# Running sums of squares by adding transfers instead of GpSimd additions

## The chip, the cores and the metric

The kernel runs on one core of a Trainium2 chip. A core has five engines with instruction queues of their own: TensorE (PE in the profile; its weight loads are listed as PEld), VectorE (DVE), ScalarE (ACT), GpSimd (POOL) and SyncE (SP, which here only issues transfers). The metric is the device time of one execution in microseconds; the kernel before takes 1895.79 us.

## The reference

A decoder trunk of two layers over 512 tokens of width 1024. Each layer has a channel mixer, a token mixer and a second channel mixer, each behind a norm of its own:

```python
def rmsnorm(x, g):
    x32 = x.astype(jnp.float32)
    y = x32 * lax.rsqrt(jnp.mean(x32 * x32, axis=-1, keepdims=True) + RMS_EPS)
    return y.astype(x.dtype) * g

def swiglu(x, w_gate, w_up, w_down):
    return (jax.nn.silu(x @ w_gate) * (x @ w_up)) @ w_down

for i in range(DEPTH):                     # DEPTH = 2
    h = h + 0.5 * swiglu(rmsnorm(h, ffn_norm_a[i]), ...)
    m = rmsnorm(h, mix_norm[i])
    h = h + mixer_i(m)                     # 0: latent attention (MLA), 1: sparse attention (NSA)
    h = h + 0.5 * swiglu(rmsnorm(h, ffn_norm_b[i]), ...)
return rmsnorm(h, final_norm)
```

The hidden width of a channel mixer is 2816. Everything is float32.

## The kernel before

**Layout.** The residual stream stays in SBUF as eight chunks `h[0]` to `h[7]`, each 128 features (partitions) by 512 tokens. Products run on TensorE in three passes: each operand is split into a high part, written by ACT, and a low part, the rest, written by DVE (`split`, L173 and L174 with a gain; `wslab`, L143 and L145 for weights).

**The norm.** A norm has two halves. The gain is multiplied into the split of each chunk as soon as the chunk is done (`norm_split`). The root of the mean square comes later, as a factor on the outputs of the products, since it is one number per token. For it the squares of the eight chunks have to be added: `sumsq` squares a chunk on ACT (L250) and adds it to the running sum `s2` on POOL (L254). Then `norm_col` adds over the partitions with small matmuls into `pc` (L276), DVE takes the inverse root by Newton steps on 128x4 numbers (`newton`, L264 to L269), and `norm_bcast` spreads it over the partitions into `pb` (L288), which ACT copies to `row`.

**The order.** The chunks come out one by one at the end of the previous mixer, in `w_o1` for a token mixer (`h` by L629) and at the end of `ffn` for a channel mixer (`h` by L399). `norm_chunk` is called for each. For a norm ahead of a channel mixer (gains b0, a1, b1; `to_ffn`) the last two chunks of the order are put into `late`: their squares are taken inside the next `ffn`.

**The channel mixer.** `ffn(idx, ...)` goes over 22 blocks of 128 hidden features. The first three (`PLAIN`) are computed directly: block `f` has a gate projection `pg` and an up projection `pu`, both by `plain` (L362 to L364), 48 matmuls each. From the fourth block on seven products stand in place of eight; `wsums` loads its weights (`rg` by L315, `ru` by L317) and `combine` builds the sums of activations for them, with ACT copies `y` (L232) and DVE differences `u` (L236 to L238). The root is needed after the two projections of the second block, where `row` enters the gates. The call `late()` in `ffn` adds the last two squares and calls `norm_col`: for `idx` 1 behind the up projection of the first block, for `idx` 2 and 3 between its two projections. `idx` 0 takes its root in another way.

**Memory and queues.** Squares are written to a scratch tile `sq`. In the token mixers it shares six buffers with the attention's `p` tiles; in `ffn` it has one buffer. Each mixer has memory pools of its own, which are opened when it begins and given back when it ends, so the first tiles of a mixer lie where the previous mixer's tiles were. Each engine takes its instructions in one fixed order. That order is not the order of the text: the build draws it from the dependences and its own estimates of durations, and breaks ties by the order of the text.

Transfers are issued by SP (weights) and ACT (constants, output); POOL issues none. In this kernel POOL adds squares, makes some low parts during the attention and scales probabilities.

Of the kernel before, what the change touches and what calls it, by code (L numbers as in the profile page):

```python
# [11 lines left out]
F32 = mybir.dt.float32  # L12
F32R = mybir.dt.float32r
I32 = mybir.dt.int32
AF = mybir.ActivationFunctionType
ALU = mybir.AluOpType
AX = mybir.AxisListType

P = 128
S = 512  # L20
D = 1024
# [40 lines left out]
class Kern:  # L62
# [112 lines left out]

    def norm_begin(self, gain):
        self.ng = GAINS[gain] if gain else None
        self.xh, self.xl, self.s2, self.late = [], [], None, []
        self.to_ffn = gain in FGAINS
        self.nng = 8 * FGAINS.index(gain) if self.to_ffn else None  # L180
        self.xc = {}

        self.order = [c + KP * e for c in range(KP) for e in range(2)] if self.to_ffn and gain != "a0" else list(range(KC))

    def norm_chunk(self, c):

        self.norm_split(c)
        if self.to_ffn and c in self.order[-2:]:

            self.late.append(c)  # L190
        else:
            self.sumsq(self.h[c], self.s2 is None)

    def norm_split(self, c):
        t = self.xp.tile([P, 2 * S], F32R, tag="x", bufs=KC, name="x")
        if self.to_ffn:

            g = self.ngains[:, self.nng + c : self.nng + c + 1]
            v = t.rearrange("p (e z n) -> p e z n", e=2, z=2)
            hi, lo, src = v[:, :, 0, :], v[:, :, 1, :], self.h[c].rearrange("p (e n) -> p e n", e=2)  # L200
            self.split(src, hi, lo, gain=g)
            for e in range(2):
                self.xc["LR"[e], c] = v[:, e, 0, :], v[:, e, 1, :]
        else:
            self.split(self.h[c], t[:, :S], t[:, S:], gain=self.gains[:, self.ng + c : self.ng + c + 1])
            self.xh.append(t[:, :S])
            self.xl.append(t[:, S:])
# [157 lines left out]

    def ffn(self, idx, gain_next, ap, tp):
        nc, a = self.nc, self.a
        self.scr, self.fp = (tp, "sq", 1), tp
        ah, al, ht, row = {}, {}, [], None
        tg, tu, units = {}, {}, []  # L370

        def gate(f, g):

            t = tg[f] = tp.tile([P, S], F32, tag="tg", bufs=2, name="tg")
            nc.vector.tensor_tensor(t, g, row, op=ALU.mult)
            nc.scalar.activation(t, t, AF.Silu, scale=-1.0)
            nc.vector.tensor_tensor(t, t, row, op=ALU.mult)
# [4 lines left out]
        def act(f):  # L382
            t = tu[f]
            if f < PLAIN:
                t = tu_tile()
                nc.vector.scalar_tensor_tensor(t, tu[f], -1.0, tg[f], op0=ALU.mult, op1=ALU.mult)
            else:
                nc.vector.tensor_tensor(t, t, tg[f], op=ALU.mult)
            ah[f] = ap.tile([P, S], F32R, tag="act", bufs=4 * NG, name="ah")
            al[f] = ap.tile([P, S], F32R, tag="act", bufs=4 * NG, name="al")  # L390
            self.split(t, ah[f], al[f])
# [21 lines left out]
        def tokens(t):  # L413

            xts.append(tp.tile([P, D], F32, tag="fr", bufs=3, name="xt"))
            with self.tc.issue_after(self.high.ins):
                nc.scalar.dma_start(xts[t], a["x_tok"][t * P : (t + 1) * P, :])

        def squares(t):
            nc.scalar.activation(xts[t], xts[t], AF.Square, accum_out=sums[:, t : t + 1])  # L420

        def late():
            for c in self.late:
                self.sumsq(self.h[c])
            return self.norm_col(D, self.s2)

        if idx == 0:
            for t in range(3):
                tokens(t)


        gates = [self.bank("T", "pg") for _ in range(PLAIN)]
        for f, g in enumerate(gates):
            u = tu[f] = self.bank(("mm", "S")[f % 2], "pu")
            self.plain(idx, f, 0, g)
            if f == 0 and idx > 1:
                col = late()
            if f == 1 and idx == 0:

                squares(0)  # L440
                tokens(3)
                squares(1)
            self.plain(idx, f, 1, u)
            if f == 0 and idx == 1:

                col = late()
            if f == 1:
                if idx == 0:
                    squares(2)
                    squares(3)  # L450
                    col = self.rsqrt_col(sums, D)
                pb = self.norm_bcast(col)
                row = tp.tile([P, S], F32, tag="row", bufs=1, name="row")
                nc.scalar.activation(row, pb, AF.Copy)
                for e in range(2):
                    gate(e, gates[e])
                    act(e)
            elif f:
                gate(f, g)
                act(f)  # L460
            for p in (((0,), (1,), (2, 3)) if idx else ((0, 1), (2,), (3,)))[f]:
                self.combine(p)
# [875 lines left out]
```

## Time and profile before

| | |
|---|---|
| median of three runs | 1895.79 us |
| fastest run | 1895.11 us |
| span of the profiled execution | 1891.5 us |
| own time of the profiled execution | not listed; median less span is 4.3 us |
| TensorE busy | 1865.3 us, 99% of the span |
| VectorE busy | 1527.3 us, 81% |
| ScalarE busy | 1091.4 us, 58% |
| GpSimd busy | 291.8 us, 15% |
| additions of squares on GpSimd (L254) | 38, mean 1441 ns, 54.8 us |

How to read the rows. In a timeline: start and duration in us, engine, line of the code, operation, output tile `<-` input tiles, shapes, count; in brackets how long the engine stood idle before it and what released it. A row of a group gives the count, the total time, the mean of one in ns, and the idle time before. In a windows table each engine's busy time stands with its number of instructions. `SPq` is SyncE's queue of transfers. Matmuls overlap in TensorE's pipeline, so their durations are longer than the distance of their starts.

### The profile page before, as it was taken

To read this page: it belongs to the slowest core of one execution; us is meant where nothing else is said; L and a number is where in the kernel's file an instruction comes from. 1 tells how busy PE (TensorE), PEld (TensorE's weight loads), DVE (VectorE), ACT (ScalarE), POOL (GpSimd) and SP (SyncE) were. 2 spreads that over 40 slices of the span, in tenths; PEclk is the share of its full clock that TensorE was granted. 3 is DMA by queue.
4 is the path that set the end of the run, shared out by engine and by line. 5 is a ranking of instruction groups with operands and counts; after the bars stand their busy time and mean duration, and the time that the engine had idled before them with its cause. 6 is when DMAs were issued, how large, how long until landed. Compare 5 with 4: busy or idle time off the path is not lost.

```text
span 1891.5 us, 33006 instructions
## 1 busy us (share of the span) xinstructions
PE 1865.3 (99%) x12510; PEld 1696.1 (90%) x12510; DVE 1527.3 (81%) x2884; ACT 1091.4 (58%) x2031; POOL 291.8 (15%) x351
## 2 busy tenths in 40 slices
PE   8999999999999999999999999999999999999998
PEld 8999999878879999998999999988788889999997
DVE  8988886677779888886988888666988989888885
ACT  7555554478756555554655555435887866555553
POOL 0000000257720000001100000032666530000000
PEclk9999999999999999999999999999999999999999
DMA  6433331311133333322433332143122133333321
GB/s 231 138 101 100 103 99 41 112 54 46 59 105 117 113 108 105 101 75 60 162 105 101 108 113 87 43 148 106 57 65 70 34 120 117 110 107 107 102 77 67
DMA packets 75903, 183.26 MB, mean 97 GB/s; under 512 B 9041, under 2 KB 37073, under 8 KB 75745
## 3 DMA queue, kind: packets, MB, share of 16 engines
q1 hardware_dynamic: 72800, 176.39, 29.7%
q10 hardware_dynamic: 2944, 4.77, 0.7%
q8 instruction: 98, 1.61, 0.4%
q14 instruction: 61, 0.49, 0.1%
HBM read 178.96 MB, written 2.16 MB: 96 GB/s over the span
## 4 chain that ended last, share of the span: by engine, by line
PE 85%; DVE 7%; ACT 5%; issue 2%; POOL 1%; DMA 1%; SPq 0%; DVEq 0%; ACTq 0%; POOLq 0%
PE pd L163 8%; PE pd L162 8%; PE pd L164 8%; PE px L350 5%; PE px L351 5%; PE px L352 5%; PE pg L350 4%; PE pg L352 4%; PE pg L351 4%; PE pq L352 4%; PE pq L350 4%; PE pq L351 4%; ACT p L643 1%; PE o L1149 1%; PE po L162 1%
## 5 line engine op out<-in xcount | busy, mean ns | idle before, releaser
L163 PE MATMUL pd<-al,wd 128*128 128x512 f32 x576 | 225.0, 391 | 0.0
L162 PE MATMUL pd<-ah,wd 128*128 128x512 f32 x576 | 224.8, 390 | 0.0
L164 PE MATMUL pd<-ah,wd 128*128 128x512 f32 x576 | 224.6, 390 | 0.0
L254 POOL TENSOR_TENSOR s<-s,sq 128x512 f32<-128x512 f32 x38 | 54.8, 1441 | 1062.6 <-ACT sq L250 1059.5
L171 DVE TENSOR_TENSOR w<-wr,w 128x1024 fp32r<-128x1024 f32 x72 | 88.1, 1224 | 135.5 <-ACT w L170 135.5
L350 PE MATMUL px<-four,wh 128*128 128x256 f32 x608 | 168.6, 277 | 0.1
L352 PE MATMUL pq<-four,wl 128*128 128x256 f32 x608 | 167.9, 276 | 0.3 <-DVE wl L171 0.3
L352 PE MATMUL px<-four,wl 128*128 128x256 f32 x608 | 168.0, 276 | 0.0
L350 PE MATMUL pq<-four,wh 128*128 128x256 f32 x608 | 167.9, 276 | 0.0
L351 PE MATMUL px<-four,wh 128*128 128x256 f32 x608 | 167.9, 276 | 0.0
L351 PE MATMUL pq<-four,wh 128*128 128x256 f32 x608 | 167.8, 276 | 0.0
L399 DVE SCALAR_TENSOR_TENSOR h<-pd,h 128x512 f32<-128x512 f32 x216 | 147.5, 683 | 13.9 <-PE pd L164 13.8
L143 ACT ACTIVATE w<-wr 128x1024 fp32r<-128x1024 f32 (+5 forms) x120 | 100.6, 844 | 97.5 <-issue 19.6
L170 ACT ACTIVATE wd<-wdr 128x384 fp32r<-128x384 f32 x192 | 99.2, 519 | 98.5 <-ACT wd L170 63.0
L164 PEld LDWEIGHTS pd<-ah,wd 128*128 128x128 f32 x576 | 108.2, 188 | 22.9
L162 PEld LDWEIGHTS pd<-ah,wd 128*128 128x128 f32 x576 | 108.1, 188 | 20.3
L163 PEld LDWEIGHTS pd<-al,wd 128*128 128x128 f32 x576 | 108.1, 188 | 19.6
L145 DVE TENSOR_TENSOR w<-wr,w 128x1024 fp32r<-128x1024 f32 (+4 forms) x81 | 84.2, 1041 | 49.2 <-ACT w L143 48.5
L643 ACT ACTIVATE p<-p,small 128x512 f32<-128x512 f32 (+2 forms) x192 | 106.5, 556 | 19.8 <-DVE small L642 16.9
L171 DVE TENSOR_TENSOR wd<-wdr,wd 128x384 fp32r<-128x384 f32 x192 | 105.2, 550 | 14.8 <-ACT wd L170 13.9
L350 PEld LDWEIGHTS px<-four,wh 128*128 128x128 f32 x608 | 114.1, 188 | 1.3 <-ACT pg L481 0.8
L170 ACT ACTIVATE w<-wr 128x1024 fp32r<-128x1024 f32 x72 | 76.5, 1062 | 66.4 <-PE pg L352 62.4
(348 smaller groups left out, 6243.9 us busy)
## 6 DMA issues: line engine op xcount, KB each, us to landing
wr<-in_w_gu SPq DMA_DIRECT2D x96, 512.0 KB, 3.3
ru<-in_w_gu SPq DMA_DIRECT2D x76, 512.0 KB, 4.1
wdr<-in_w_down SPq DMA_DIRECT2D x192, 192.0 KB, 2.4
wr<-in_w_down SPq DMA_DIRECT2D x24, 256.0 KB, 2.6
wr<-in_mla_w_o SPq DMA_DIRECT2D x8, 512.0 KB, 3.3
wr<-in_nsa_w_q SPq DMA_DIRECT2D x8, 512.0 KB, 3.3
th<-btab_d SPq DMA_DIRECT2D x16, 256.0 KB, 3.5
wr<-in_nsa_w_o SPq DMA_DIRECT2D x8, 512.0 KB, 3.5
```

Source lines behind the costliest of these rows:

```text
L143: self.copied = nc.scalar.activation(wh[:, m], raw[:, m], AF.Copy)
L145: nc.vector.tensor_tensor(wl[:, m], raw[:, m], f32v(wh[:, m]), op=ALU.subtract)
L162: mm(out, wh, xh, start=first, stop=False)
L163: mm(out, wh, xl, start=False, stop=False)
L164: return mm(out, wl, xh, start=False, stop=last)
L170: nc.scalar.activation(hi, src, AF.Copy)
L171: (nc.gpsimd if pool else nc.vector).tensor_tensor(lo, src, f32v(hi), op=ALU.subtract)
L350: mm(out, wh[:, p], xh, start=first and p == 0, stop=False, skip_group_check=True)
L351: mm(out, wh[:, p], xl, start=False, stop=False, skip_group_check=True)
L352: mm(out, wl[:, p], xh, start=False, stop=last and p == KP - 1, skip_group_check=True)
L399: nc.vector.scalar_tensor_tensor(self.h[c], p, 0.5, self.h[c], op0=ALU.mult, op1=ALU.add)
L643: nc.scalar.activation(p_sb[:, :n], p_sb[:, :n], AF.Exp, bias=nm, scale=-1.0, accum_out=sm)
```

## The change

The three norms ahead of channel mixers that follow another mixer (b0, a1, b1) no longer use `sumsq`. A new `squares` keeps two running sums, `sums2[0]` and `sums2[1]`. The first square of each is written straight into it by ACT. Each further square goes to a scratch tile, and a transfer issued by POOL, with `accum_op=add`, adds it to one of the two sums in turn. The two late squares are moved to the head of the next `ffn`, ahead of its first weights. `late()` adds the two sums on DVE and calls `norm_col`; for `idx` 2 and 3 the call moves from between the projections of the first block to behind them, where it already stood for `idx` 1. The scratch tile in `ffn` gets three buffers in place of one. The norms ahead of the token mixers, and those inside MLA, keep `sumsq`.

```diff
     def norm_begin(self, gain):
         self.ng = GAINS[gain] if gain else None
-        self.xh, self.xl, self.s2, self.late = [], [], None, []
+        self.xh, self.xl, self.s2, self.late, self.nsq = [], [], None, [], 0
         self.to_ffn = gain in FGAINS
         self.nng = 8 * FGAINS.index(gain) if self.to_ffn else None
-        self.xc = {}
+        self.xc, self.sums2 = {}, []
...
             self.late.append(c)
+        elif self.to_ffn:
+            self.squares(c)
         else:
             self.sumsq(self.h[c], self.s2 is None)
+
+    def squares(self, c):
+
+        nc, z = self.nc, self.nsq % 2
+        self.nsq += 1
+        if len(self.sums2) < 2:
+            self.sums2.append(self.sp.tile([P, S], F32, tag="s2", bufs=2, name="s2"))
+            nc.scalar.activation(self.sums2[z], self.h[c], AF.Square)
+        else:
+            sq = self.scratch("sq")
+            nc.scalar.activation(sq, self.h[c], AF.Square)
+            nc.gpsimd.dma_start(self.sums2[z], sq, accum_op=ALU.add)
...
     def ffn(self, idx, gain_next, ap, tp):
         nc, a = self.nc, self.a
-        self.scr, self.fp = (tp, "sq", 1), tp
+        self.scr, self.fp = (tp, "sq", 3), tp
...
         def late():
-            for c in self.late:
-                self.sumsq(self.h[c])
-            return self.norm_col(D, self.s2)
+            nc.vector.tensor_tensor(self.sums2[0], self.sums2[0], self.sums2[1], op=ALU.add)
+            return self.norm_col(D, self.sums2[0])
...
+        for c in self.late if idx else []:
+            self.squares(c)
         gates = [self.bank("T", "pg") for _ in range(PLAIN)]
         for f, g in enumerate(gates):
             u = tu[f] = self.bank(("mm", "S")[f % 2], "pu")
             self.plain(idx, f, 0, g)
-            if f == 0 and idx > 1:
-                col = late()
...
             self.plain(idx, f, 1, u)
-            if f == 0 and idx == 1:
-
+            if f == 0 and idx:
                 col = late()
```

## The prediction

> **What bounds the kernel now.** I read the head of the page first, then the group of the instructions that the change replaces, then three windows around the three norms that it touches.
>
> ```profile
> span 1891.5 us, 33006 instructions
> ...
> PE 1865.3 (99%) x12510; PEld 1696.1 (90%) x12510; DVE 1527.3 (81%) x2884; ACT 1091.4 (58%) x2031; POOL 291.8 (15%) x351
> ...
> L254 POOL TENSOR_TENSOR s<-s,sq 128x512 f32<-128x512 f32 x38 | 54.8, 1441 | 1062.6 <-ACT sq L250 1059.5
> ```
>
> TensorE is busy for 1865.3 of 1891.5 us. Whatever the change does, it can give back at most the idle 26.2 us, 1.4% of the span, and only the share of it that stands near a norm. The POOL additions cost 54.8 us in all, but POOL is idle for most of the span: their own time is on nobody's path.
>
> ```profile
> core 0: us, PE busy (x) PEld busy (x) DVE busy (x) ACT busy (x) POOL busy (x), PEclk, DMA share, GB/s
> 545.00:592.00 47.00, 44.37 (x309) 40.32 (x307) 42.18 (x63) 31.87 (x45) 10.22 (x7) 1.00 0.44 143
> 882.00:930.00 48.00, 46.98 (x323) 43.05 (x322) 40.02 (x65) 32.38 (x47) 10.55 (x7) 1.00 0.50 163
> 1526.00:1570.00 44.00, 43.96 (x314) 40.72 (x313) 40.33 (x63) 32.49 (x45) 9.98 (x7) 1.00 0.48 163
> ```
>
> These are the norms ahead of the second, third and fourth channel mixer (I call them b0, a1 and b1 after their gains). TensorE is idle for 2.63, 1.02 and 0.04 us there, 3.69 us together. That is the ceiling of the gain. The timeline of TensorE in these windows names each gap in its last column:
>
> ```profile
> 561.55 0.39 PE L364 MATMUL pg<-x,w 128*128 128x256 f32 x1 [0.58 <-DVE w L145]
> 566.74 0.38 PE L362 MATMUL pg<-x,w 128*128 128x256 f32 x1 [0.35 <-ACT x L173]
> 567.78 0.38 PE L363 MATMUL pg<-x,w 128*128 128x256 f32 x1 [0.66 <-DVE x L174]
> 573.94 0.94 PE L276 MATMUL pc<-ones,s 128*128 128x1 f32 x8
> 575.45 0.39 PE L364 MATMUL pg<-x,w 128*128 128x256 f32 x1 [0.22 <-DVE w L145]
> 581.95 0.39 PE L364 MATMUL pu<-x,w 128*128 128x256 f32 x1 [0.77 <-DVE w L145]
> ...
> 903.07 0.39 PE L364 MATMUL pg<-x,w 128*128 128x256 f32 x1 [0.75 <-DVE w L145]
> 908.27 0.39 PE L363 MATMUL pg<-x,w 128*128 128x256 f32 x1 [0.27 <-DVE x L174]
> 908.98 0.95 PE L276 MATMUL pc<-ones,s 128*128 128x1 f32 x8
> 926.24 1.05 PE L288 MATMUL pb<-ident,small 128*128 128x128 f32 x8
> ```
>
> The matmuls that read the sum (pc, L276) and those that spread its root (pb, L288) carry no gap: the norm itself is never late. The gaps are waits for VectorE's splits of weights (L145) and of the activations (L174). Why is VectorE late there? Its own rows, two by line for 530 to 600 us (min/median/max) and four by time:
>
> ```profile
> L174 DVE SCALAR_TENSOR_TENSOR x<-h,ngains,x x8: 737/752/1774, 548.4 to 567.0; 128x512 fp32r<-128x512 f32 x8
> ...
> L145 DVE TENSOR_TENSOR w<-wr,w x9: 1209/1220/1700, 538.0 to 588.6; 128x1024 fp32r<-128x1024 f32 x9
> ...
> 555.32 1.77 DVE L174 SCALAR_TENSOR_TENSOR x<-h,ngains,x 128x512 fp32r<-128x512 f32 x1
> 559.96 1.53 DVE L145 TENSOR_TENSOR w<-wr,w 128x1024 fp32r<-128x1024 f32 x1
> 561.42 1.77 DVE L174 SCALAR_TENSOR_TENSOR x<-h,ngains,x 128x512 fp32r<-128x512 f32 x1
> ...
> 906.44 1.78 DVE L174 SCALAR_TENSOR_TENSOR x<-h,ngains,x 128x512 fp32r<-128x512 f32 x1
> ```
>
> ```profile
> 554.94 1.60 POOL L254 TENSOR_TENSOR s<-s,sq 128x512 f32<-128x512 f32 x1 [0.63 <-ACT sq L250]
> 561.26 1.38 POOL L254 TENSOR_TENSOR s<-s,sq 128x512 f32<-128x512 f32 x1 [0.85 <-ACT sq L250]
> ...
> 898.71 1.34 POOL L254 TENSOR_TENSOR s<-s,sq 128x512 f32<-128x512 f32 x1 [1.37 <-ACT sq L250]
> 903.01 1.82 POOL L254 TENSOR_TENSOR s<-s,sq 128x512 f32<-128x512 f32 x1 [2.97 <-DVE w L145]
> ```
>
> The long L174 instructions (1.77 beside a median of 0.75) lie over POOL additions: 555.32 beside 554.94, 561.42 beside 561.26. The addition at 903.01 was held 2.97 us by VectorE in its turn. So the two engines hold each other up when both read two operands, and in b0 that costs VectorE 1.02 + 0.31 + 1.02 = 2.35 us in the row of instructions that ends in the gaps 0.58, 0.35 and 0.66.
>
> **What the change removes.** Each touched norm loses seven POOL additions (window column POOL: x7), 21 of the 38. In b0 the three gaps sum to 1.59 us; 2.35 us of VectorE delay stand ahead of them, so I count all 1.59 as gone. The two later gaps, 0.22 and 0.77, come from a VectorE that works off its backlog; it is relieved, but gets a new addition (below), so I count half, 0.50. In a1 the 0.27 hangs on the long instruction at 906.44 and goes. In b1 TensorE has no gap to lose.
>
> The squares change no count: eight ACT squares per norm before and after. The buffer of the squares in the mixers grows from one to three. The one wait that this ends is the 0.47 in the second row here, ACT time behind which no TensorE gap stands; I cost it at nothing.
>
> ```profile
> 568.90 0.63 ACT L250 ACTIVATE sq<-h 128x512 f32<-128x512 f32 x1 [0.47 <-POOL s L254]
> ...
> 898.01 0.62 ACT L250 ACTIVATE sq<-h 128x512 f32<-128x512 f32 x1
> 900.08 0.72 ACT L232 ACTIVATE y<-h,gains 128x512 f32<-128x512 f32 x1 [1.45 <-POOL s L254]
> 900.71 1.04 ACT L143 ACTIVATE w<-wr 128x1024 fp32r<-128x1024 f32 x1
> ```
>
> **What it adds.** Six transfers per norm, 18 in all, issued by POOL, each 256 KB from SBUF into SBUF with an addition. The trace has no transfer issued by POOL and none that adds, so I bound the time L from the end of the square to the landing by the nearest transfers (last column: us to landing):
>
> ```profile
> th<-btab_d SPq DMA_DIRECT2D x16, 256.0 KB, 3.5
> ...
> h<-in_x SPq DMA_DIRECT2D x8, 256.0 KB, 5.0
> ...
> out_t<-four SPq DMA_DIRECT2D x4, 256.0 KB, 2.0
> ...
> w<-in_nsa_w SPq DMA_DIRECT2D x2, 0.5 KB, 8.3
> ```
>
> Between 2.0 (256 KB out of SBUF) and 8.3 us (the slowest kind in the program) I take 3.5, the row of the same size in the middle of the kernel. The Trainium skill, page "DMA: Bandwidth & Descriptors", section on the anatomy of one DMA on the gpsimd path, gives such a transfer about 2.0 us plus its bytes at 436 GB/s; for 256 KB that is an estimate of 2.6 us by the page. No run here shows it yet; by it the release worked out next would come 1.2 us later than now, not 2.1.
>
> First new wait: the old scratch memory. In a1 the copy y (L232), the first write into the new mixer's memory, waits until 900.05 for the POOL addition of the sixth square (898.71 + 1.34); so does the load rg. In b0 rg follows the addition that ends at 562.64.
>
> ```profile
> 562.66 0.33 SPq L315 DMA_DIRECT2D rg<-in_w_gu  x1
> ...
> 900.07 0.33 SPq L315 DMA_DIRECT2D rg<-in_w_gu  x1
> ```
>
> After the change both wait for a landing: in a1 898.63 + 3.5 = 902.1, that is 2.1 us later. Queued behind y on ACT is the weight copy of 900.71, on which the gap of 0.75 hangs; behind rg on SP are ru and the next weight loads. If the build keeps that order, a1 loses 2.1 us. But y stands far behind the weight copy in the program's text and was drawn ahead when the build took it for ready early; with a later release I expect the weight copy ahead. Then the 0.75 shrinks, but the first late square, which the new code puts ahead of this copy, may take its place on ACT (0.62 us, on the row of 898.01). I count 0.23 of the 0.75, with the 0.27 a gain of 0.50 in a1. In b0 rg moves to 561.26 + 3.5 = 564.8, with ru behind it; VectorE's first sum that uses ru is this:
>
> ```profile
> 571.24 0.68 DVE L336 TENSOR_TENSOR s<-ru 128x512 f32<-128x512 f32 x1
> ...
> 910.69 0.14 DVE L259 TENSOR_SCALAR small<-pc 128x4 f32<-128x4 f32 x1
> ...
> 919.71 0.15 DVE L269 SCALAR_TENSOR_TENSOR small<-small 128x4 f32<-128x4 f32 x1
> ```
>
> 564.8 plus 5.0 for a load in traffic is 569.8, ahead of 571.24: hidden.
>
> Second: one VectorE addition per norm, 0.68 us by L336, three of them. It is hidden by VectorE's idle time in the windows (47.00 - 42.18 = 4.8 us, 8.0, 3.7). It waits for both chains, and behind it on VectorE stand the weight splits of the next gate and the Newton steps. In b0, even with the last square left at 568.90: 569.53 + 3.5 + 0.68 = 573.7, just ahead of the pc matmuls at 573.94. The square now stands ahead of the two y copies (0.72 us each by L232) and loses its wait of 0.47, which gives it 1.9 us more.
>
> Third: the root later. In a1 and b1 pc moves behind the second projection. The Newton steps took from 910.69 to 919.86, 9.2 us. Three projections lie between pc at 908.98 and pb at 926.24, 5.75 us each with pc's own share; moved by one of them the steps end near 925.6, with pb wanted at 926.24: 0.6 us to spare. Nothing is lost, nothing gained, since pc had no gap.
>
> **Sum.** The executions differ from the span by what lies around it: 1895.8 (median) less 1891.5 is 4.3 us, and the page gives no other own time for the profiled one. 1.59 + 0.50 + 0.50 + 0 = 2.6 us: 1895.8 - 2.6 = **1893.2**.
>
> **The rivals.**
>
> *B, order kept.* L is 3.5, and y stays ahead of the weight copy: b0 gives 2.1, a1 gives 0.27 and takes 2.1. 1895.8 - 0.3 = **1895.5**. For it: the drawn order of 900.08 before 900.71. Against: that order rests on an early release.
>
> *C, transfers slow (slower).* One mechanism: each transfer must wait for the one before in its chain, and y, rg and pc wait for the last. With the order kept it decides from L = 3.8 (898.63 + 3.8 - 900.05 eats the 2.4 gained); with the order changed from 573.94 - 0.68 - 569.53 + 1.9 = 5.6, when pc in b0 begins to wait. At 5.0 with the order kept, a1 loses 3.6: 1895.8 - 2.4 + 3.6 = 1897. At 8.3: in a1 the fourth square ended 5.4 us before the sixth (spacing 1.37 + 1.34), at 893.2; it lands at 901.5, the sixth goes out then and lands at 909.8, 9.75 late. In b0 the fourth ended at 554.9 and lands at 563.2, the sixth at 571.5, the eighth at 579.8, plus 0.68: pc 6.5 late. With 6.5 for b1 too: 22.8 - 2.4 = 20, **1916**. For it: no row shows such a transfer. Against: only tiny loads took 8.3.
>
> *D, the relief is not passed on.* The gaps are VectorE's load and not POOL's hold; freed time goes to the next instruction, and the gaps stay: **1895.8**. Against: the 1.77 beside 0.75. The transfers could also hold VectorE as the additions did. The Trainium skill, page "SBUF — State Buffer", section "Who interferes with whom", says that VectorE with two SBUF inputs is held by a POOL instruction that reads SBUF, and infers that making descriptors needs the write side only. The first half agrees with the 1.77; no run here shows the second.
>
> **How the numbers follow.** My forecast 0.50, B 0.20, C 0.20, D 0.10. Forecast's own spread: 1892.1 (all 3.69 gained) to 1895. The range drops the upper half of C, at 1903 and above, and a little below the floor, since executions differ by some tenths: 1891.5 to 1903. A measurement of this kernel tells about 2% (38 us) from no change. Faster by that is more than the idle 26.2 us: 0.01. Slower needs L well above 8.3: 0.04. Within: 0.95.
>
> **What would show it.** Right: L174 near 0.75 and L145 near 1.22 throughout 545 to 592, the gaps 0.58, 0.35 and 0.66 gone, seven POOL additions fewer in each window, pc and pb without a gap, landings under 4 us. Wrong: a gap on pg for L145 of 2 us and more near 903 with y ahead of it (B); a gap on pc or a VectorE wait for a transfer (C); L174 still at 1.77 (D). A different order drawn by the build in the stages between could also shift the time, by amounts that this trace can't bound.

## The result: slower by 1.1%, and the profile after

The changed kernel takes 1915.07 us (median of 4 runs, 1914.29 to 1918.64) beside 1895.68 us for the kernel before in the same comparison. The ratio is 1.0109, 95% interval 1.0094 to 1.0124: some 19 us lost where a gain of 2.6 was forecast, and rival C's story. Three runs took far longer (4826.06 us of the kernel before here, 2659.91 in experiment 5, 10701.99 in experiment 10); they count in the medians, and no ratio uses them. Lines below stand 12 to 14 lower in the new code: `pc` is L290, `pb` L302, the plain products L376 to L378, `y` L246; new are the squares L205, the transfers L206 and VectorE's joining addition L437.

From the page of the changed kernel, the parts on the span, the queues and the groups:

```profile
span 1914.0 us, 33053 instructions
...
PE 1873.7 (98%) x12510; PEld 1704.3 (89%) x12510; DVE 1520.8 (79%) x2887; ACT 1090.8 (57%) x2031; POOL 276.3 (14%) x348
...
q1 hardware_dynamic: 72800, 176.39, 29.8%
q0 software_dynamic: 2592, 4.72, 1.4%
...
L268 POOL TENSOR_TENSOR s<-s,sq 128x512 f32<-128x512 f32 x17 | 23.9, 1403 | 699.0 <-ACT sq L264 699.0
```

The span grew by 22.5 us in the profiled execution. TensorE does the same 12510 matmuls; its busy time grew by 8.4 us and its idle time from 26.2 to 40.3, by 14.1. So there are two losses to explain: waits, and matmuls that run slower. (All other executions here last some 1.8 us longer than their span. By that, an estimate, the profiled execution of the kernel before took about 1893.3 us, less than any in the comparison, and the traces lie some 3 us farther apart than the medians.) The additions went from 38 to 17 as the change says, and queue q0 is new: 18 transfers with 4.72 MB.

The waits of the changed kernel over the stretch with the three norms (540 to 1640 us; total, times, longest), those that bear on the norms:

```profile
DVE s L437 <- DMA s<-sq: 16.4, 3, 6.0
...
ACT sq L205 <- DMA s<-sq: 8.8, 3, 3.4
...
PE pc L290 <- DVE s L437: 6.8, 3, 2.9
...
POOL s L206 <- DMA s<-sq: 5.0, 2, 3.0
...
PE pg L378 <- DVE w L145: 3.8, 4, 1.2
...
PE px L364 <- ACT pg L493: 3.4, 2, 2.0
...
PE pg L377 <- DVE x L174: 2.5, 3, 0.9
```

Read from the causes to TensorE: the joining addition waits for landings at each of the three norms, 16.4 us in all, and `pc` waits for it. The weight split L145 stands behind the same addition on VectorE, and `pg` (L378) waits for that. The late squares wait for a landing as well, and they stand ahead of the weight copy L143 on ACT; so that copy, VectorE's splits behind it and `pg` (L377) wait too. With 0.9 us for `pb` and 0.4 for `pg` at L376, TensorE's waits at the norms sum to 17.8 us. In the kernel before they sum to 3.7; the difference is the 14.1 us of idle time. Here is the order in b0, chosen rows of the timeline (SyncE, ACT, POOL, VectorE, TensorE):

```profile
563.59 0.33 SPq L329 DMA_DIRECT2D rg<-in_w_gu  x1
563.62 0.63 ACT L205 ACTIVATE sq<-h 128x512 f32<-128x512 f32 x1 [3.41 <-DMA s<-sq]
563.96 0.43 SPq L331 DMA_DIRECT2D ru<-in_w_gu  x1
564.15 1.04 ACT L143 ACTIVATE w<-wr 128x1024 fp32r<-128x1024 f32 x1
564.61 0.86 POOL L206 DMA_DIRECT2D s<-sq  x1 [3.56 <-ACT sq L205]
566.48 0.33 SPq L140 DMA_DIRECT2D wr<-in_w_gu  x1
566.68 0.86 POOL L206 DMA_DIRECT2D s<-sq  x1 [1.21 <-ACT sq L205]
566.86 1.00 SPq L331 DMA_DIRECT2D ru<-in_w_gu  x1
567.17 0.39 PE L377 MATMUL pg<-x,w 128*128 128x256 f32 x1 [0.93 <-DVE x L174]
574.54 0.69 DVE L437 TENSOR_TENSOR s<-s,s 128x512 f32<-128x512 f32 x1 [4.89 <-DMA s<-sq]
575.37 1.02 PE L290 MATMUL pc<-ones,s 128*128 128x1 f32 x8 [1.86 <-DVE s L437]
576.68 1.22 DVE L145 TENSOR_TENSOR w<-wr,w 128x1024 fp32r<-128x1024 f32 x1
577.96 0.58 PE L378 MATMUL pg<-x,w 128*128 128x256 f32 x1 [1.22 <-DVE w L145]
```

At 563.6 the sixth square's transfer lands and the old scratch memory comes free. That one landing lets go both the late squares on ACT, which write the new mixer's memory, and the loads on SyncE, which had piled up behind `rg`. So the last two transfers go out at 564.6 and 566.7 into the middle of four weight loads. The stretch 564 to 577 by queue and by issue (MB and share of the 16 engines; median us to landing), then the six transfers of this norm by tile:

```profile
q1 hardware_dynamic: 576, 2.10, 48.3%
q0 software_dynamic: 288, 0.52, 22.1%
...
ru<-in_w_gu SPq DMA_DIRECT2D x2, 512.0 KB, 6.6
s<-sq POOLq DMA_DIRECT2D x2, 256.0 KB, 6.7
wr<-in_w_gu SPq DMA_DIRECT2D x1, 512.0 KB, 7.2
```

```profile
L206 POOL DMA_DIRECT2D s<-sq x6: 857/868/1026, 551.6 to 566.7; - x6
...
DMA to landing us min/median/max: 3.3/5.1/7.8
```

Two transfers hold 22% of the engines for a quarter of the loads' bytes, and everything lands late: the loads `ru` after 6.6 us, the transfers after 5.7 and 7.8. POOL spends 0.86 us to issue one. In a1 the last two took 8.1 and 8.0 us, in b1 5.5 and 8.7.

Then the second loss. The columns here are those of the windows: busy time and count by engine, granted clock, DMA share.

```profile
576.00:578.00 2.00, 0.78 (x7) 0.58 (x6) 2.00 (x4) 2.00 (x4) 0.00 (x0) 0.81 0.00 0
578.00:580.00 2.00, 2.00 (x9) 2.00 (x10) 2.00 (x5) 0.40 (x1) 0.00 (x0) 0.50 0.46 147
580.00:585.00 5.00, 5.00 (x29) 5.00 (x28) 5.00 (x12) 2.95 (x3) 0.00 (x0) 0.59 0.17 57
```

Behind the gaps of 1.86 and 1.22 us the granted clock falls to 0.50, for 6.83 us by the trace's clock records. In that stretch a matmul starts every 0.213 us, where the running stream has one every 0.114. The same happens for 6.83 us in a1 and for 3.41 twice in b1: 20.5 us at half clock. Before had none at a norm. TensorE counts as busy there: 84 matmuls start in the four stretches, and 0.1 us for each is about 8 us, which is the 8.4 us of busy time, nearly.

By the starts of the n-th matmul against before, each norm taken with the stretch behind it, b0 loses 3.9 us, a1 7.2 and b1 11.3.

### The profile page after: what moved, and what is told of

It is laid out like the page before. It is cut to its first block, busy times and chain, and to the rows that moved or that the text cites. A ratio compares the mean times of both kernels' runs of the same rounds, so it can differ in the third digit from the quotient of the medians.

```text
span 1914.0 us, 33053 instructions
## 1 busy us (share of the span) xinstructions
PE 1873.7 (98%) x12510; PEld 1704.3 (89%) x12510; DVE 1520.8 (79%) x2887; ACT 1090.8 (57%) x2031; POOL 276.3 (14%) x348
## 3 DMA queue, kind: packets, MB, share of 16 engines
q0 software_dynamic: 2592, 4.72, 1.4%
## 4 chain that ended last, share of the span: by engine, by line
PE 81%; DVE 7%; ACT 5%; DMA 3%; issue 2%; POOL 1%; SPq 0%; ACTq 0%; DVEq 0%; POOLq 0%
PE pd L163 8%; PE pd L164 8%; PE pd L162 8%; PE px L364 5%; PE px L365 5%; PE px L366 5%; PE pg L364 4%; PE pg L365 4%; PE pg L366 4%; PE pq L366 4%; PE pq L365 4%; PE pq L364 4%; DMA s<-sq 2%; ACT p L655 2%; PE o L1161 1%
## 5 line engine op out<-in xcount | busy, mean ns | idle before, releaser
L143 ACT ACTIVATE w<-wr 128x1024 fp32r<-128x1024 f32 (+5 forms) x120 | 100.6, 844 | 105.8 <-issue 24.3
L413 DVE SCALAR_TENSOR_TENSOR h<-pd,h 128x512 f32<-128x512 f32 x216 | 147.8, 684 | 13.7 <-PE pd L164 13.6
L145 DVE TENSOR_TENSOR w<-wr,w 128x1024 fp32r<-128x1024 f32 (+4 forms) x81 | 82.7, 1023 | 57.3 <-ACT w L143 56.7
L268 POOL TENSOR_TENSOR s<-s,sq 128x512 f32<-128x512 f32 x17 | 23.9, 1403 | 699.0 <-ACT sq L264 699.0
L366 PEld LDWEIGHTS pq<-four,wl 128*128 128x128 f32 x608 | 114.2, 188 | 0.7 <-DVE wl L171 0.7
```

The lines of the kernel that those rows point to most:

```text
L143: self.copied = nc.scalar.activation(wh[:, m], raw[:, m], AF.Copy)
L145: nc.vector.tensor_tensor(wl[:, m], raw[:, m], f32v(wh[:, m]), op=ALU.subtract)
L366: mm(out, wl[:, p], xh, start=False, stop=last and p == KP - 1, skip_group_check=True)
L413: nc.vector.scalar_tensor_tensor(self.h[c], p, 0.5, self.h[c], op0=ALU.mult, op1=ALU.add)
```

## The experiments

Each edit is against the changed kernel unless it says otherwise, and each ratio is against runs of the kernel before beside it.

**1. POOL's additions, the rest of the change kept.**

```diff
-            nc.gpsimd.dma_start(self.sums2[z], sq, accum_op=ALU.add)
+            nc.gpsimd.tensor_tensor(self.sums2[z], self.sums2[z], sq, op=ALU.add)
```

> One line of the changed kernel undone: the additions are made by POOL again, everything else (two chains, late squares first, root half a block later, VectorE's last addition, three buffers) stays. Theory T (the transfers cost the time: the last two land some 8 us after their issue, VectorE's addition L437 and with it TensorE wait for them, and TensorE's clock halves after the gaps): back to the kernel before, 1894 to 1898 us, no halved clock outside the tail. Rival O (the new places of the squares, the root and the addition cost it): stays within 4 us of 1915. Rival M (old memory is released by a landing) says the same as T here.

Measured: 1896.14 us, ratio 1.0011 (1.0002 to 1.0021). The transfers cost some 19 us; the two chains, the joining addition, the late squares ahead and the later root, together with POOL's additions in these places, cost 2. One stretch of 3.41 us at half clock, which was not expected, stands in b0 behind a gap of 2.2 us on L174. VectorE's rows of the activation splits around b0 (530 to 600 us, by line; min/median/max in ns) show what the transfers took away. This kernel:

```profile
L174 DVE SCALAR_TENSOR_TENSOR x<-h,ngains,x x8: 741/751/1786, 548.7 to 566.8; 128x512 fp32r<-128x512 f32 x8
```

The changed kernel:

```profile
L174 DVE SCALAR_TENSOR_TENSOR x<-h,ngains,x x8: 742/746/753, 547.9 to 566.4; 128x512 fp32r<-128x512 f32 x8
```

With POOL adding, the longest takes 1.79 us, with POOL issuing transfers none is above 0.75. VectorE's relief is real, and issuing does not hold it.

**2. The transfers left out with nothing in their place.** Six of the eight squares are not in the sum; it prices the relief.

```diff
-            nc.gpsimd.dma_start(self.sums2[z], sq, accum_op=ALU.add)
```

> The changed kernel without the transfers and with nothing in their place: six of the eight squares of the three norms are computed but not added (this leaves out most of the sum). It shows what all relief is worth: no POOL addition beside VectorE and no transfer to wait for. My prediction's credits (1.59 + 0.50 + 0.50) say 2.6 us below the kernel before. Rival D (the gaps are VectorE's own load): within 1 us of before. If it is above before, the new places of squares and addition cost by themselves.

Measured: 1888.39 us, ratio 0.9969 (0.9958 to 0.9981), 5.7 us faster. The windows of b0, a1 and b1:

```profile
545.00:592.00 47.00, 47.00 (x345) 44.20 (x344) 40.57 (x68) 33.57 (x48) 0.00 (x0) 1.00 0.46 148
882.00:930.00 48.00, 48.00 (x354) 45.23 (x353) 42.36 (x71) 34.84 (x52) 0.00 (x0) 1.00 0.53 174
1526.00:1570.00 44.00, 44.00 (x338) 41.83 (x338) 36.72 (x63) 31.23 (x44) 0.00 (x0) 1.00 0.48 164
```

No gap is left. In b0 345 matmuls stand where before had 309. That is worth 4.4 us by their starts, though before's idle time there was 2.6: in the running stream a matmul starts 0.114 us after the one before (median step of the starts), but is drawn some 0.28 long, and the idle time of a gap is counted only from the drawn end. By distances of starts, before's five gaps in b0 cost 0.86 + 0.63 + 1.04 + 0.50 + 1.05 less five times 0.114, which is 3.5 us. By the starts a1 gains another 1.7 us and b1 loses 0.8. One thing moved besides: the sum hangs on the two squares that are ready first, and in a1 the build drew `pc` behind 2 matmuls of the mixer and not behind 96. So the 5.7 us need not be the relief alone.

**3. Plain transfers, without the addition** (the sum holds only the squares copied last). It parts the addition inside a transfer from the transfer.

```diff
-            nc.gpsimd.dma_start(self.sums2[z], sq, accum_op=ALU.add)
+            nc.gpsimd.dma_start(self.sums2[z], sq)
```

> The same 18 transfers issued by POOL, from and to the same memory, but plain copies without the addition (the sum then holds two squares only). If the addition inside the transfer makes it slow: landings fall to 2 to 4 us also beside the weight loads, and the time to 1896 to 1902 us. If it is the crowd of loads and POOL's way of issuing: landings of the late two stay at 6 to 9 us and the time within 3 us of the changed kernel (1912 to 1917).

Measured: 1904.80 us, ratio 1.0052 (1.0037 to 1.0067). The queue on its page:

```profile
q0 software_dynamic: 1440, 4.72, 0.6%
```

Its transfers in b0, by tile (ns of one issue, then us to landing):

```profile
L206 POOL DMA_DIRECT2D s<-sq x6: 536/536/735, 552.5 to 566.4; - x6
...
DMA to landing us min/median/max: 2.5/4.0/5.3
```

Its waits between 540 and 1640 us:

```profile
PE pb L302 <- DVE small L283: 4.9, 3, 1.8
PE px L364 <- ACT pg L493: 4.0, 2, 2.0
```

The same bytes go in 1440 packets instead of 2592 and take 0.6% of the engines' time instead of 1.4%; the issue is 0.54 us instead of 0.86, the longest landing in b0 5.3 instead of 7.8. `pc` waits only 0.5 us, and no norm meets a halved clock. Neither of the two forecasts came true: about half of the loss is due to the addition inside the transfer, its longer issue included. The other half stays with a plain copy: the joining addition still waits 9.5 us for landings, and the lateness comes out at `pb`. Of the waits at `px`, 3.2 us stand also where nothing is late (experiment 10).

**4. Scratch memory of its own** for the squares, two buffers that no mixer's memory waits for.

```diff
-            sq = self.scratch("sq")
+            sq = self.sp.tile([P, S], F32, tag="sq2", bufs=2, name="sq")
...
-        self.scr, self.fp = (tp, "sq", 3), tp
+        self.scr, self.fp = (tp, "sq", 1), tp
```

> The changed kernel with the squares' scratch in memory of its own (two buffers) instead of the old mixer's pool, so that no first write of the new mixer waits for a landing. Rival M (the release by a landing makes the late squares 2.4 to 3.4 us late and bunches the loads with the last transfers): the waits of the late squares for a transfer go, the last two transfers land in 4 to 5 us, pc waits under 0.5 us, 1895 to 1899 us. Theory T: the last transfers still meet the weight loads, but start some 3 us earlier; pc waits 0 to 1 us per norm, 1900 to 1908 us. If the time stays above 1912, the release has no part.

Measured: 1903.60 us, ratio 1.0053 (1.0036 to 1.0070), in theory T's span, so about half of the loss hangs on the release of the old memory. a1 is free of it: its longest landing is 5.5 us in place of 8.1, and by the starts of matmuls it gains 0.8 where the change lost 7.2. b1 loses 5.6 in place of 11.3. b0 keeps its loss (3.7); its longest landing is 9.2 and the late squares now wait for a scratch buffer instead. Of the halved clock 6.83 us stay in b0 and as much in b1.

**5. No joining addition**: `pc` takes both sums, with eight small matmuls more per norm.

```diff
-            nc.tensor.matmul(pc[:, i : i + 1], s2[...], ..., start=True, stop=True)
+            ss = s2 if isinstance(s2, list) else [s2]
+            for k, s in enumerate(ss):
+                nc.tensor.matmul(pc[:, i : i + 1], s[...], ..., start=(k == 0), stop=(k == len(ss) - 1))
...
-            nc.vector.tensor_tensor(self.sums2[0], self.sums2[0], self.sums2[1], op=ALU.add)
-            return self.norm_col(D, self.sums2[0])
+            return self.norm_col(D, self.sums2)
```

> The changed kernel without VectorE's addition: the matmuls into pc take both sums, one after the other (0.8 us more of TensorE per norm). Theory T with VectorE's queue as the place (the weight splits behind L437 wait with it): TensorE waits for the landing itself, 1 to 2 us per norm, but the gap of 0.9 to 1.2 us for the next weight split goes and with it half or more of the halved clock: 1903 to 1909 us. If TensorE's own wait for the landing is what counts: 1912 to 1916.

Measured: 1904.88 us, ratio 1.0053 (1.0036 to 1.0070). Its waits:

```profile
PE pc L292 <- DMA s<-sq: 3.1, 3, 1.3
```

`pc` still waits for the landing, though 3.1 us instead of 6.8, and behind the weight split 0.3 us of gaps are left of 3.8. About half of the loss thus goes through VectorE standing still with weight splits behind it. The halved clock shrinks from 20.5 us to one stretch of 3.41.

**6. Both: own memory and no joining addition.**

> Memory of its own for the squares and no addition on VectorE (both sums into pc). Each alone gave back about half of the loss. If the two parts are different waits (release of the old memory; VectorE's queue behind the addition): together 1895 to 1898. If they remove the same wait twice: 1901 to 1904, as each alone.

Measured: 1898.08 us, ratio 1.0022 (1.0013 to 1.0032). The two edits saved 0.0056 each alone and save 0.0087 together: mostly different waits, with some overlap. `pc` still waits 3.8 us for two landings, one of them 11.5 us after its issue.

**7. The late two squares added by POOL, the early four by transfers.**

```diff
+            if self.nsq > 6:
+                nc.gpsimd.tensor_tensor(self.sums2[z], self.sums2[z], sq, op=ALU.add)
+            else:
+                nc.gpsimd.dma_start(self.sums2[z], sq, accum_op=ALU.add)
```

> The first four transferred squares of a norm stay transfers, the two late ones are added by POOL. Theory T (the last two transfers are what is late): 1895 to 1900 us, pc without a gap, but the late squares still wait for the release of the old memory by a landing (2.4 to 3.4 us on ACT). Rival M: that wait alone costs 2 us and more per norm, 1901 to 1908.

Measured: 1903.89 us, ratio 1.0053 (1.0038 to 1.0068). Its waits:

```profile
PE pg L380 <- DVE x L174: 4.8, 3, 2.2
...
ACT sq L205 <- DMA s<-sq: 8.9, 3, 3.7
```

`pc` has no gap, yet half of the loss remains: the late squares wait for the early transfers' landings as before, and then POOL holds VectorE again, at the new mixer's first matmuls. Each norm has a stretch of 3.41 us at half clock.

**8. TensorE kept busy through the gap** by 24 useless matmuls ahead of `pc`, against the halved clock.

```diff
+        for i in range(24 if self.to_ffn and self.sums2 else 0):
+            nc.tensor.matmul(pc[:, :HS], self.ones, self.xc["LR"[i % 2], i % KC][0], start=True, stop=True, skip_group_check=True)
```

> The changed kernel with 24 matmuls of no use ahead of the ones into pc (2.7 us of TensorE at full clock), so that TensorE works while it would wait for the addition; results unchanged. If the halved clock after the gaps is a cost of its own: the 20.5 us of halved clock at the norms shrink to under 7, and the time falls to 1904 to 1909 although work was added. If the halved clock costs nothing because TensorE waits anyway: 1915 or more.

Measured: 1917.92 us, ratio 1.0118 (1.0101 to 1.0135). This expectation failed: the time does not differ from the changed kernel's beyond the intervals. The wait at `pc` went from 6.8 to 0.7 us, but 24 matmuls at the usual step of 0.114 us are 2.7 us per norm, 8.2 in all, 2 more than they fill; `pb` then waits 3.9 us; and four stretches of 3.41 us at half clock remain, 13.6 us. The sum is as late as before, so what TensorE does in the meantime saves nothing. What the halved clock alone costs isn't parted by a run; the 8.4 us of busy time is a reading of the trace.

**9. The sum wanted where before wanted it**: for a1 and b1 `late()` again between the first two projections, transfers kept.

```diff
+            if f == 0 and idx > 1:
+                col = late()
...
-            if f == 0 and idx:
+            if f == 0 and idx == 1:
```

> After with the norm's matmuls of the two later norms (a1, b1) back between the first and the second projection, half a block earlier; transfers kept. Theory 1 (pc waits for the landing of the last two transfers, which does not depend on the place of pc): in a1 and b1 the wait grows by up to one projection, 5.75 us each, from 2.06 and 2.92 to 6 to 8.7 us; 1915 + 8 to 11 = 1921 to 1927, with pb's waits gone. Rival 2 (the build draws late squares and transfers earlier when the sum is wanted earlier, so that place hardly counts): 1913 to 1917.

Measured: 1921.23 us, ratio 1.0140 (1.0125 to 1.0155). Its waits:

```profile
PE pc L290 <- DVE s L437: 15.9, 3, 7.0
DVE s L437 <- DMA s<-sq: 15.7, 3, 5.4
```

Theory 1 holds. The landing stays where it is (15.7 beside 16.4 us of VectorE's wait) and the gap on `pc` grows from 6.8 to 15.9. At half clock stand 34.1 us in place of 20.5. The half block is worth 6 us to the transfers; it is not enough for them.

**10. VectorE's additions**, the rest of the change kept.

```diff
-            nc.gpsimd.dma_start(self.sums2[z], sq, accum_op=ALU.add)
+            nc.vector.tensor_tensor(self.sums2[z], self.sums2[z], sq, op=ALU.add)
```

> After with its six transfers per norm replaced by VectorE additions (18 in all, 0.68 us each by the row of L437); places of the squares, buffers and VectorE's joining addition as in after. Theory 1 (what costs time is waiting for landings; VectorE has the room, 5 to 8 us idle in each norm's window): the additions lie in VectorE's idle time, the hold by POOL stays away, pc waits under 1 us, no stretch of halved clock at b0 and a1: 1890 to 1895, that is at or a little below before, between the 1888.4 with no additions at all and the 1896.1 with POOL's. Rival 2 (VectorE has no room where it counts: its additions push the weight splits as POOL's hold did): 6 x 0.68 = 4.1 us of VectorE per norm, most of it passed on: 1896 to 1901.

Measured: 1892.78 us, ratio 0.9992 (0.9983 to 1.0002). The time is inside theory 1's span. The windows:

```profile
545.00:592.00 47.00, 47.00 (x347) 44.33 (x346) 43.86 (x74) 33.60 (x48) 0.00 (x0) 1.00 0.45 148
882.00:930.00 48.00, 48.00 (x355) 45.24 (x355) 43.23 (x75) 32.36 (x48) 0.00 (x0) 1.00 0.52 170
1526.00:1570.00 44.00, 44.00 (x332) 41.57 (x330) 39.51 (x69) 30.83 (x44) 0.00 (x0) 1.00 0.50 166
```

The additions lie in VectorE's idle time: no gap in any window. Part of what is lost against experiment 2 shows behind the windows, in its waits, where the products `px` of the fourth block stand still for 3.2 us:

```profile
PE px L364 <- ACT pg L493: 3.2, 2, 2.4
```

That the later root brings this wait is not shown: `pb` has no gap here, and in a1 `row` follows 1.2 us behind it, as in the kernel before.

**11. Early four transfers from memory of their own, late two on VectorE** (the edits of 4 and 7, with `nc.vector` for the late two).

> After with transfers for the early four squares of each norm only (12 in all), their scratch in memory of its own (two buffers that no mixer's memory waits for), and the late two added by VectorE (0.68 us each). Theory 1 (the loss sits in the late two transfers and in the release of the old scratch memory; the early four land in 3.3 to 6 us with nobody waiting): both waits go; pc without a gap, no halved clock, VectorE pays two additions more per norm: 1890 to 1895. Rival 2 (the early transfers cost by themselves, through the loads that they slow and POOL's issue, or the squares now wait for a scratch buffer until a landing): 1897 to 1901, with ACT waits for s<-sq landings or late weight loads on the page.

Measured: 1897.14 us, ratio 1.0016 (1.0006 to 1.0025). Rival 2: even the early transfers cost. From its waits:

```profile
ACT sq L205 <- DMA s<-sq: 8.4, 4, 5.1
```

A square's buffer stays taken until its transfer lands, so with two buffers the squares queue for landings. By the starts b0 loses 1.1 us, where experiment 10, with VectorE's additions, gains 4.4. The early transfers and their two buffers are not parted here.

**12. The kernel before, with one edit**: VectorE adds in the three norms.

```diff
-            nc.gpsimd.tensor_tensor(self.s2, self.s2, sq, op=ALU.add)
+            (nc.vector if self.to_ffn and self.ng != GAINS["a0"] else nc.gpsimd).tensor_tensor(self.s2, self.s2, sq, op=ALU.add)
```

> Before with one edit: in the three norms ahead of the mixers, the seven additions of each are made by VectorE (0.68 us each) and not by POOL; one chain, the last two squares, the sum's matmuls and the order of the code all as in before. It parts the change's moves (late squares ahead, sum wanted half a block later) from the choice of the engine. Theory 1 (POOL's hold of VectorE made the gaps, and the moves are worth about nothing): TensorE's gaps in the windows 545 to 592 and 882 to 930, 3.65 us, go at least by half, and the time is that of the kernel with VectorE additions and the moves kept, 0.9992 of before: 1890 to 1894. Rival 2 (the moves are what lets VectorE's additions hide): the last two additions, now behind squares that ACT reaches only between the projections, hold the weight splits or pc; gaps on pg behind L145 or on pc: 1895 to 1901. Rival 3 (the moves cost, as the 2 us of the kernel with POOL's additions and the moves hint): 1887 to 1890.

Measured in five rounds: 1890.47 us, ratio 0.9981 (0.9972 to 0.9990): faster than both kernels, by 3.6 us against before. Its windows of b0 and a1:

```profile
545.00:592.00 47.00, 47.00 (x345) 44.20 (x344) 43.59 (x74) 33.69 (x48) 0.00 (x0) 1.00 0.44 148
882.00:930.00 48.00, 48.00 (x353) 45.13 (x352) 44.24 (x77) 33.42 (x49) 0.00 (x0) 1.00 0.53 174
```

The one gap in b1, from its timeline:

```profile
1545.22 1.02 PE L276 MATMUL pc<-ones,s 128*128 128x1 f32 x8 [0.49 <-DVE s L254]
```

Seven additions of 0.68 us by VectorE itself are cheaper than the same seven on POOL. The moves of the change don't help here: with them the ratio is 0.9992 on VectorE and 1.0011 on POOL, without them 0.9981 and 1. Both differences, 0.0011, are near the intervals' half widths, but they agree on some 2 us against the moves; rival 3 named the direction, theory 1 the time. The starts of the matmuls show where: in b0, where the sum keeps its place, experiment 10 gains 4.4 us and this kernel 4.3; in a1 and b1, where the sum moves, experiment 10 loses 0.2 and 1.1, and this kernel gains 1.0 and loses 0.3. By what way the later sum costs this stays open.

## Why the prediction was wrong

**The step that failed is L**, the time from a square to its landing. It was taken as 3.5 us, from loads in the middle of the kernel. The early transfers begin near it (3.2 to 6.0 us from the issue). The late two, on which `pc` hangs, took 5.5 to 8.7. From the end of the square, as the prediction has L, it is 3.6 to 6.3 for the early and 5.9 to 9.2 for the late. Two reasons were not in the working. The late transfers go out together with the loads that the previous landing released, so a single quiet row was the wrong neighbour. And a transfer that adds costs more than its bytes: 1.4% against 0.6% of the engines' time. The Trainium skill, page "DMA: Bandwidth & Descriptors", section on the anatomy of one DMA, gives about 2.0 us plus the bytes at 436 GB/s, an estimate of 2.6 us for 256 KB; by it the release would have come even earlier than by the 3.5. All 18 landings, 3.2 to 8.7 us, are above it; the plain copies of experiment 3 begin near it (2.3 to 6.6).

**Old scratch memory.** The prediction let `rg`, `y` and what stands behind them wait for a landing, and called b0 hidden and a1 worth a gain of 0.50. The waiting instructions were named rightly, but the first to wait is the late square on ACT, which the change itself puts ahead, and with it the next landing. The working priced this square by its own 0.62 us in front of the weight copy; it holds the copy for its wait of 2.4 to 3.4 us as well. That is rival B's way of losing time, with the square in the place of `y`. Own memory (4) gives back about half of the loss.

**The joining addition** was called hidden, with 1.9 us to spare in b0. Hidden was its 0.68 us; not hidden was its wait of 4.9 to 6.0 us, during which VectorE does nothing and the weight splits queue behind it. The working had named that queue and priced only the addition. Experiment 5 shows its share.

**The root later** had 0.6 us to spare. With the lateness it is overrun: `pb` waits 0.9 us in b1. The 3.4 us at `px` can't be put down to the lateness, since 3.2 stand in experiment 10 too. Experiments 9, 10 and 12 part the two sides: half a block more helps the transfers by 6 us, and costs about 2 where nothing is late.

**The halved clock** was no term at all. Some 8 us of the loss lie there, as the trace reads; no run parts them from the gaps.

**The relief** was right in its mechanism and too small: L174 is at 0.75 and POOL has no addition left in the windows, as said. Credited were 2.6 us; experiment 2 gave 5.7, in which the early sum of a1 may have a part. The ceiling of 3.69 us was wrong, since idle time by the drawn ends of matmuls understates a gap. Rival D is out.

**Rival C** came true, and at its far end: 1916 for L of 8.3, against 1915. Its sum was not that of the runs, though. It let each transfer wait for the one before in its chain; POOL waits so for 5.0 us in all, two times, and the late landings are slow by their addition and beside the loads. It made a1 the dearest norm, and b1 was; it had 20 us of waiting, and the trace has 14 of idle time and 8 of slow clock. The time met the price partly by chance, and its chance of 0.20 with a range that ended at 1903 left it out.

## What to carry to other kernels

A transfer in place of a small engine instruction trades a sure microsecond for a landing of 3 to 9, and takes its buffer, its reader and the memory behind it along: before such a move, list all that will wait for the landing, and price it by the transfers beside which it will run. When two engines hold each other up, moving the work onto the one that is held can be the cheaper cure: look first for its idle time in that stretch. Price a gap by the distance of starts, and gaps of some microseconds on TensorE also by the clock that follows.

## What the runs showed of the hardware

Adding inside a transfer between two places in SBUF: 144 packets for 256 KB where a plain copy has 80 (2592 and 1440 over 18), 2.3 times the engines' time, and 0.86 us of issue on POOL instead of 0.54.

The clock of TensorE halved behind gaps of 1.9 to 2.9 us with others close by, for 3.41 or 6.83 us at a time in the changed kernel. In experiment 11 three gaps of 0.66, 0.89 and 1.18 us within five microseconds brought one stretch of 3.41, while single gaps of 1.8 and 2.0 us in experiment 3 brought none. The Trainium skill, page "TensorE: Matmul & The Clock Gate", section on the HAM clock gate, has a window of 3.4 us and warns of idle gaps above that: the length of the stretches agrees, but no gap at a norm of the changed kernel was above 2.9 us.

What decides between two gaps of 2 us can be read from the traces. Before the end of the kernel they hold 20 halved stretches, four of them in the changed kernel and 16 in the experiments. Each begins a whole number of steps of 3.413 us after the first entry in the clock record of its trace, and where these steps lie in the kernel differs from run to run. Count in each step the share that drawn matmuls cover, without those into `pc`, which have a single column. Of the steps at full clock, those just ahead of a halved stretch were covered for 0 to 0.48, and one for 0.51; of all the other steps the emptiest have 0.48, 0.51 and 0.53. With the matmuls into `pc` counted, two of the 20 don't fit (0.71 and 0.78, in experiments 4 and 5). So what counted here is whether about half of one such step stood still. The same gap can fall into one step or be parted by two, and that part of the loss is luck: the emptiest steps of experiment 3 have 0.56 and 0.61.
